# A transformer block on one core: the borders between its last four stages rearranged

## The chip, the cores and the metric

The kernel runs on one core of one Trainium2 chip. The core has a matrix engine (TensorE, PE), a vector engine (VectorE, DVE), a scalar engine (ScalarE, ACT), GpSimd (POOL) and queues that move data between device memory and the core's SBUF; almost all DMAs here are issued on SyncE's queue (SP). The metric is the device time of one execution in microseconds (us).

## The reference, cut to what matters

One block over 2048 latent tokens of width 1024, with 256 context tokens. `mix` is made of gated linear attention (GLA) and of differential softmax attention, 512 columns each; the rest is what the change touches:

```python
mix = jnp.concatenate([gla_merge(og, r, gla_norm_g[l]),
                       diff_merge(od, diff_norm_g[l], lam_init)], axis=-1) @ w_out[l]
x = x + gt1 * mix
x = x + gt2 * swiglu(modulate(x, norm2_g[l], sh2, sc2), w_ffn_in[l], w_ffn_out[l])

def swiglu(h, w_in, w_out):
    gate, up = jnp.split(h @ w_in, 2, axis=-1)     # hidden width 2816
    return (jax.nn.silu(gate) * up) @ w_out
```

`gt1` and `gt2` are vectors over the 1024 output columns, `diff_merge` is an RMS norm over each head's 128 columns.

## The kernel before, in words

All products are float32, made of three matmuls each (`mm3`, lines 93 to 96): every operand is split into a rounded high part and a low rest by `split` (lines 89 to 91), a copy on ACT (L90) and a subtraction on DVE (L87). The elementwise helpers `mul`, `add` and `sub` have lines 81, 84 and 87, so many groups of the trace carry those lines. The order of PE's instructions is the order in which the program emits them (`manual_schedule(engines=MS)`, MS holding PE alone); the other engines' order is set by the scheduler, which takes what its own model of time says is ready, by priority, that is by place in the program.

*Attention.* 64 tiles of 128 queries (4 heads x 16); scores `s` on PE, softmax on ACT, and `combine` takes one probability map from the other (`p`): a multiply on DVE and an addition on POOL. The AV stream transposes `p`, splits it (`ah`, `al`) and multiplies with the values; its last tiles run after the last scores.

*Out-projection.* w_out's eight tiles of 128 x 1024 are loaded into buffers of the pool `xt`, multiplied by `gt1` on POOL and split into `woh`, `wol`. Token tiles lt = 15 to 0 then go through three generators. `prep(lt)` loads attention's output, merges the GLA output (state update `S` on DVE, L940), normalizes each head (ACT squares L976, DVE scalings L986 of `mx`), transposes (`tp`) and splits into `mh`, `ml`. `main(lt)` does 16 steps of three matmuls, two output halves of eight steps; after each half DVE adds the residual (`xt<-mm,xt`), which gives x1. `mod2(g)` takes two finished tiles: square on ACT (L1023), scaling to `xn` on DVE (L1025), transposes on PE and the modulation on DVE, into `hb` (SBUF) or device memory. Where each piece stands among the 16 steps of `main` is in `PREP` and `MOD`: `prep(lt-1)` is emitted at steps 0, 7 and 13 of `main(lt)`, `mod2` of the two tiles before at steps 1, 8, 10, 12 and 14 of every second one.

*Gate/up.* A Strassen-like scheme: each pair of 128 hidden columns of gate and up over 1024 tokens (one item, n) is seven products of 12 matmuls each, from seven weight combinations (`weights`, split into `wh`, `wl`) and seven activation slots (`slots`, o0 to o6, split into `o0h`, `o0l`, ...). `finish` combines the seven results with DVE additions (`e`) and ACT copies and Silus, and stores to device memory (`act`). There are 44 items, 22 on each half of the tokens; the slots are built once for each half by `rebuild`, in items 0 and 21. Four of the seven products add into an accumulator bank that a product before has left there:

```python
SEQ_P = ((0, True), (1, True), (0, False), (2, True), (3, True), (2, False), (3, False))
```

The second column says whether a product opens its bank; before product 2 adds into bank 0, the result of product 0 must have been copied (`e1`, ACT), and before products 5 and 6 the sums of products 3 and 4 must have been made (DVE). `last_group` normalizes and modulates tiles 0 and 1 during item 1.

*Down projection.* 16 pairs of token tiles; for a pair, 22 hidden tiles of six matmuls. Weights are loaded as `wo` (raw, `wrp`), split to `wot` (`wop`) by `down_weights`; token chunks are loaded as `ar` and split to `ah`, `al` by `tokens`. A second set of weights (the other 512 output columns) is prepared in pairs 5 and 7.

Pools are placed in SBUF one after the other, and a pool's memory comes free when the tiles before it in that place have been read, so the order of the pools decides what a transfer waits for.

Of the kernel before, what the change touches and what calls it, by code (L numbers as in the profile page):

```python
# [11 lines left out]
F32 = mybir.dt.float32  # L12
# [22 lines left out]
ORD0, ORD1 = (4, 5, 6, 7, 0, 1, 2, 3), (3, 2, 4, 5, 6, 7, 0, 1)  # L35
PAD4 = 16
# [5 lines left out]
MS = {mybir.EngineType.PE}  # L42
BKL = (3, 6, 9, 12)
# [9 lines left out]
def dit_block(ctx: ExitStack, tc: tile.TileContext, x, c, cx, c_ctx, w_mod, b_mod, norm1_g, w_in, gate_up,  # L53
# [651 lines left out]

    with ExitStack() as st:
# [55 lines left out]
        def score_stream():  # L762
            later, ring = [], iter(range(64))
            for bi, (h, qb, i0, nq) in enumerate(blocks):
                as_[bi] = []
                for i in range(i0, i0 + nq):
# [5 lines left out]
                    for c_ in range(2):  # L772
                        mx = sm.tile([P, 5], F32, name="mx", tag="mx")
                        for j, (o0, n) in enumerate(CH):
# [5 lines left out]
                            if j == len(CH) - 1:  # L780
# [5 lines left out]
                                if c_ == 1:  # L786
                                    later.append([CD, combine(pr, ls)])
# [9 lines left out]
        def combine(pr, ls):  # L797
            def go():
# [13 lines left out]
        def av_stream():  # L812
            ats, po, ending = {}, None, []
            NB = len(blocks) * NKT
            for p in range(NB + LOOK + 4):
# [21 lines left out]
                if 0 <= a < NB:  # L837
# [55 lines left out]
    with ExitStack() as st:  # L893
        st6 = st.enter_context(ExitStack())
        h2p = st6.enter_context(tc.tile_pool(name="s45h", bufs=1, reuse_waits="tile"))
# [11 lines left out]
        pad = st1.enter_context(tc.tile_pool(name="s4pad", bufs=1, side="right"))  # L907
        G.memset(pad.tile([P, 56], F32, name="pad"), 0.0)
        gl = st1.enter_context(tc.tile_pool(name="s4g", bufs=2, side="right", reuse_waits="tile"))
        pp = st1.enter_context(tc.tile_pool(name="s4p", bufs=2, side="right", reuse_waits="tile"))  # L910
        pad = st1.enter_context(tc.tile_pool(name="s4pad2", bufs=1, side="right"))
        G.memset(pad.tile([P, PAD4], F32, name="pad"), 0.0)
# [3 lines left out]
        xp = st1.enter_context(tc.tile_pool(name="s4x", bufs=4, reuse_waits="tile"))  # L916
# [3 lines left out]
        gt1 = ph.tile([P, D], F32, name="gt1", tag="mh")  # L920
# [44 lines left out]
        def prep(lt):  # L965
# [3 lines left out]
            xt = xp.tile([P, D], F32, name="xt", tag="xt")  # L969
            load(xt, x[0, lt * P:(lt + 1) * P, :])  # L970
            gla_out(lt, mx[:, 0:512])
            sq = pp.tile([P, P], F32, name="sq", tag="sq", bufs=1)
# [14 lines left out]
            mh = ph.tile([P, KT, P], F32R, name="mh", tag="mh")  # L987
            ml = ph.tile([P, KT, P], F32R, name="ml", tag="ml")
# [28 lines left out]
        def mod2(g):  # L1017
            b, o0 = (g % 4) // 2, (g % 2) * 256
            xn = []
            for t in range(2):  # L1020
                n_t = wk.tile([P, D], F32, name="xn", tag="xn")
# [3 lines left out]
                V.tensor_scalar(out=n_t, in0=x1s[2 * g + t], scalar1=rs, scalar2=None, op0=ALU.mult)  # L1025
                xn.append(n_t)
            yield
            for kp in range(KT // 2):
# [4 lines left out]
                else:  # L1033
                    ht = wk.tile([P, 2, 256], F32, name="ht", tag="ht")
# [43 lines left out]
        pad = st6.enter_context(tc.tile_pool(name="s5pad", bufs=1, side="right"))  # L1078
        G.memset(pad.tile([P, 56], F32, name="pad"), 0.0)
# [240 lines left out]
```

## Time and profile before

| | |
|---|---|
| median of 3 runs | 3119.8 us (3116.95 to 3121.58) |
| profiled execution | 3118.64 us |
| its span | 3116.9 us, 41971 instructions |
| PE busy in the span | 3023.3 us (97%) |
| mean granted clock of TensorE | 0.988 of full speed |

The profile is of one execution; its times are from the span's start. PE is the matmul, PEld the loading of weights into the array beside it. A wait is idle time of an engine, with what ended it; a tile is named as in the program, buffer numbers left out, so `xt<-xt,gt` is an instruction that writes a buffer of `xt` and reads `xt` and `gt`. The granted clock has two levels, 1.2 and 2.4 GHz; 1.00 in a window is 2.4 GHz throughout.

### The profile page before, as it was taken

What the parts mean: (1) busy time and instruction counts of PE and PEld (TensorE: products, weight loads), DVE (VectorE), ACT (ScalarE), POOL (GpSimd) and SP (SyncE); (2) the same over time, 40 slices, a digit from 0 to 9 for tenths busy, and PEclk for the clock granted to TensorE, in tenths of its full rate; (3) what the DMA queues carried; (4) which work ended last, traced back from release to release, by engine and by line L of the source; (5) the groups of instructions that cost most, each with busy time, mean ns of one, the idle gap of its engine ahead of it and who ended that gap; (6) DMA issues with size and microseconds to landing.
All of it is one profiled execution on the core that took longest, in us unless ns stands there. A gap on an engine that the chain in (4) does not pass through costs nothing. (4 is left out here: it accounts for less than half of the span.)

```text
span 3116.9 us, 41971 instructions
## 1 busy us (share of the span) xinstructions
PE 3023.3 (97%) x15124; PEld 2486.5 (80%) x15124; DVE 2203.2 (71%) x4820; ACT 1411.9 (45%) x2195; POOL 495.6 (16%) x304
## 2 busy tenths in 40 slices
PE   7999999999989999999799899999999998999999
PEld 4888889888867777777588788888788887888887
DVE  7878667888889999999777676666766665424232
ACT  5333466666657777777434333333433333212121
POOL 2111100000046555555411000000000000000000
PEclk9999999999999999999899999999999999999999
DMA  8866511121141313121455442233233223545331
GB/s 310 291 236 220 177 66 67 60 95 64 53 130 35 90 35 90 35 75 28 135 180 171 150 144 82 83 88 89 86 89 89 84 81 124 192 144 175 120 134 68
DMA packets 319555, 363.47 MB, mean 117 GB/s; under 512 B 25842, under 2 KB 256691, under 8 KB 312691
## 3 DMA queue, kind: packets, MB, share of 16 engines
q1 hardware_dynamic: 316754, 351.36, 35.4%
q0 software_dynamic: 2304, 8.39, 0.8%
q8 instruction: 119, 1.95, 0.3%
q10 hardware_dynamic: 288, 1.05, 0.1%
q14 instruction: 90, 0.73, 0.1%
HBM read 249.96 MB, written 110.76 MB: 116 GB/s over the span
## 5 line engine op out<-in xcount | busy, mean ns | idle before, releaser
L84 POOL TENSOR_TENSOR p<-p,p 128x1152 f32<-128x1152 f32 x128 | 366.0, 2879 | 286.9 <-DVE p L808 124.6
L778 DVE TENSOR_SCALAR_CACHE_REDUCE p<-s 128x512 f32<-128x512 f32 (+1 forms) x640 | 381.8, 629 | 13.5 <-PE s L777 9.5
L94 PE MATMUL mm<-wh,hh 128*128 128x512 f32 (+2 forms) x976 | 379.0, 388 | 0.0
L96 PE MATMUL mm<-wh,hl 128*128 128x512 f32 (+2 forms) x976 | 355.1, 364 | 0.2 <-DVE hl L87 0.2
L95 PE MATMUL mm<-wl,hh 128*128 128x512 f32 (+2 forms) x976 | 354.1, 363 | 0.0
L84 DVE TENSOR_TENSOR e<-p,e 128x512 f32<-128x512 f32 x220 | 152.0, 691 | 225.7 <-PE p L96 225.4
L784 ACT ACTIVATE p<-p,nm 128x2304 f32<-128x2304 f32 x128 | 283.8, 2217 | 44.5 <-DVE nm L782 44.5
L776 PE MATMUL s<-k,qh 128*128 128x512 f32 (+1 forms) x640 | 275.5, 434 | 9.2 <-DVE p L778 8.5
L94 PE MATMUL o<-wot,ah 128*128 128x512 f32 x704 | 275.4, 391 | 6.8 <-ACT wot L90 6.1
L95 PE MATMUL o<-wot,ah 128*128 128x512 f32 x704 | 275.2, 391 | 0.9 <-DVE wot L87 0.9
L96 PE MATMUL o<-wot,al 128*128 128x512 f32 x704 | 275.0, 391 | 0.4 <-DVE al L87 0.4
L90 ACT ACTIVATE wh<-wi 128x512 fp32r<-128x512 f32 x172 | 108.4, 631 | 299.2 <-PE p L95 296.3
L777 PE MATMUL s<-k,ql 128*128 128x512 f32 (+1 forms) x640 | 234.3, 373 | 2.1 <-DMA ql<-ql 2.1
L90 ACT ACTIVATE ah<-ar 128x1408 fp32r<-128x1408 f32 x64 | 85.3, 1374 | 315.9 <-PE o L95 311.5
L96 PEld LDWEIGHTS mm<-wh,hl 128*128 128x128 f32 x976 | 184.8, 189 | 30.4 <-DVE hl L87 0.6
L94 PEld LDWEIGHTS mm<-wh,hh 128*128 128x128 f32 x976 | 186.1, 191 | 23.0 <-issue 0.5
L95 PEld LDWEIGHTS mm<-wl,hh 128*128 128x128 f32 x976 | 186.3, 191 | 21.5 <-issue 0.5
L87 DVE TENSOR_TENSOR al<-ar,ah 128x1408 fp32r<-128x1408 f32 x64 | 101.4, 1621 | 132.0 <-ACT ah L90 132.0
L90 ACT ACTIVATE wh<-s 128x512 fp32r<-128x512 f32 x129 | 81.5, 632 | 224.3 <-PE p L95 146.8
L821 PE MATMUL t<-ident,p 128*128 128x128 f32 x1152 | 174.7, 274 | 2.0 <-POOL p L84 2.0
L821 PEld LDWEIGHTS t<-ident,p 128*128 128x128 f32 x1152 | 142.7, 142 | 37.4 <-issue 4.1
L776 PEld LDWEIGHTS s<-k,qh 128*128 128x128 f32 x640 | 121.7, 190 | 59.7 <-DVE p L778 18.1
(295 smaller groups left out, 7112.2 us busy)
## 6 DMA issues: line engine op xcount, KB each, us to landing
ar<-act SPq DMA_DIRECT2D x64, 704.0 KB, 4.3
wi<-in_w_ffn_in SPq DMA_DIRECT2D x86, 512.0 KB, 5.1
act<-e SPq DMA_DIRECT2D x88, 256.0 KB, 4.2
wm<-in_w_mod SPq DMA_DIRECT2D x32, 512.0 KB, 4.9
xt<-in_x SPq DMA_DIRECT2D x30, 512.0 KB, 4.2
wr<-in_w_in SPq DMA_DIRECT2D x12, 1024.0 KB, 7.6
wo<-in_w_ffn_out SPq DMA_DIRECT2D x44, 256.0 KB, 5.3
hdh<-hh SPq DMA_DIRECT2D x9, 1024.0 KB, 4.8
```

What stands on the lines that cost most here:

```text
L84: (eng or V).tensor_tensor(out=o, in0=a, in1=b, op=ALU.add)
L87: (eng or V).tensor_tensor(out=o, in0=a, in1=b, op=ALU.subtract)
L90: S.activation(hi, src, AF.Copy)
L94: T.matmul(ps, a[0], b[0], start=start, stop=False, **how)
L95: T.matmul(ps, a[0], b[1], start=False, stop=False, **how)
L96: T.matmul(ps, a[1], b[0], start=False, stop=stop, **how)
L776: T.matmul(ps[:, 0:n], qd[0][c_][:, qc], ks_[h, c_][:, o0:o0 + n], start=True, stop=False)
L777: T.matmul(ps[:, 0:n], qd[1][c_][:, qc], ks_[h, c_][:, o0:o0 + n], start=False, stop=True)
L778: V.tensor_scalar(out=pr[c_][:, o0:o0 + n], in0=ps[:, 0:n], scalar1=1.0, scalar2=-3.0e38, op0=ALU.mult, op1=ALU.max, accum_out=mx[:, j:j + 1])
L784: S.activation(pr[c_], pr[c_], AF.Exp, bias=nm, accum_out=l)
L821: T.transpose(pt[:, i, :], as_[bi][i][:, kt * P:(kt + 1) * P], ident)
```

## The change

- *Attention to out-projection.* w_out isn't multiplied by `gt1` any more; instead `main` multiplies each output half by it (on DVE, in place in the accumulator). The raw tiles go to buffers of `xp`, `xnp` and `ph`, which lie elsewhere than before, and each split gets the priority of a place in the last AV block (`marks`). The last two `combine`s are done on DVE alone. `ORD0` and `ORD1`, the order of the steps in `main`, change.
- *Out-projection.* The squares of `prep` write into `mh` instead of a scratch; the head scalings and the `xn` scalings move from DVE to ACT.
- *Out-projection to gate/up.* The raw weights, the split weights and the temporaries of gate/up lie over buffers that come free before the out-projection's end; the first fetch and the first three weight combinations are raised in priority; the very first product does its high-by-high matmuls first and the ones with low parts after.
- *Gate/up and down projection.* `MS5` makes DVE and ACT issue in program order too.
- *Gate/up to down projection.* The first two token chunks are loaded and split in the last gate/up item; raw weight buffers go from 4 to 3, raw token buffers from 4 to 2, split weights from NH + 6 to NH + 2, x1t from 3 to 2; the second set of weights starts with 2 instead of 6 in pair 5.

```diff
-ORD0, ORD1 = (4, 5, 6, 7, 0, 1, 2, 3), (3, 2, 4, 5, 6, 7, 0, 1)
-PAD4 = 16
+ORD0, ORD1 = (4, 5, 6, 7, 3, 2, 1, 0), (0, 1, 2, 3, 4, 5, 6, 7)
 MS = {mybir.EngineType.PE}
+MS5 = {mybir.EngineType.PE, mybir.EngineType.DVE, mybir.EngineType.Activation}
...
+    marks = []
...
-                                    later.append([CD, combine(pr, ls)])
+                                    later.append([CD, combine(pr, ls, bi == len(blocks) - 1 and i >= i0 + nq - 2)])
...
-                    if e == 0:
+                    if e == 0 or last:
                         V.scalar_tensor_tensor(out=p0, in0=p1, scalar=cf, in1=p0, op0=ALU.mult, op1=ALU.add)
...
+                if p >= NB - NKT:
+                    marks.append(tc.cur_priority)
                 yield
...
-        gl = st1.enter_context(tc.tile_pool(name="s4g", bufs=2, side="right", reuse_waits="tile"))
-        pp = st1.enter_context(tc.tile_pool(name="s4p", bufs=2, side="right", reuse_waits="tile"))
...
-        ph = st1.enter_context(tc.tile_pool(name="s4h", bufs=2, side="right", reuse_waits="tile"))
+        xp = [st1.enter_context(tc.tile_pool(name=f"s4x{u}", bufs=2, side="right", reuse_waits="tile")) for u in range(2)]
+        xnp = st1.enter_context(tc.tile_pool(name="s4n", bufs=2, side="right", reuse_waits="tile"))
+        gp = st1.enter_context(tc.tile_pool(name="s4gt", bufs=1, reuse_waits="tile"))
+        htp = st1.enter_context(tc.tile_pool(name="s4ht", bufs=2, reuse_waits="tile"))
         wp = st1.enter_context(tc.tile_pool(name="s4w", bufs=1, reuse_waits="tile"))
+        ph = st1.enter_context(tc.tile_pool(name="s4h", bufs=2, reuse_waits="tile"))
+        pp = st1.enter_context(tc.tile_pool(name="s4p", bufs=2, reuse_waits="tile"))
+        gl = st1.enter_context(tc.tile_pool(name="s4g", bufs=2, reuse_waits="tile"))
...
-        for k in ORD0:
-            w = xp.tile([P, D], F32, name="xt", tag="xt")
+        for n, k in enumerate(ORD0):
+            pool, tag = {3: (xnp, "xn"), 2: (xnp, "xn"), 1: (ph, "mh"), 0: (ph, "ml")}.get(k, (xp[k // 2 % 2], "xt"))
+            w = pool.tile([P, D], F32, name="wr", tag=tag)
             load(w, w_out[0, k * P:(k + 1) * P, :])
-            mul(w, w, gt1, G)
-            split(wo[k][0], wo[k][1], w)
+            with tc.high_priority(offset=tc.cur_priority - marks[3 + 2 * n]):
+                split(*wo[k], w)
...
+            mh = ph.tile([P, KT, P], F32R, name="mh", tag="mh")
+            ml = ph.tile([P, KT, P], F32R, name="ml", tag="ml")
...
-                S.activation(sq, mx[:, 512 + h * P:512 + (h + 1) * P], AF.Square, accum_out=ss[:, h:h + 1])
+                S.activation(mh[:, h, :], mx[:, 512 + h * P:512 + (h + 1) * P], AF.Square, accum_out=ss[:, h:h + 1])
...
-                V.tensor_scalar(out=mx[:, hs], in0=mx[:, hs], scalar1=rs[:, h:h + 1], scalar2=None, op0=ALU.mult)
+                S.activation(mx[:, hs], mx[:, hs], AF.Copy, scale=rs[:, h:h + 1])
...
                     if k == order[-1]:
+                        mul(ps, ps, gt1[:, js])
                         add(x1[:, js], ps, xt[:, js])
...
-                V.tensor_scalar(out=n_t, in0=x1s[2 * g + t], scalar1=rs, scalar2=None, op0=ALU.mult)
+                S.activation(n_t, x1s[2 * g + t], AF.Copy, scale=rs)
...
+            if n == i == 0:
+                for u, v in ((wh_, 0), (wh_, 1), (wl_, 0)):
+                    for k in range(4):
+                        T.matmul(ps, u[:, k, :], slots[0][v][:, k, :], start=u is wh_ and v == k == 0,
+                                 stop=u is wl_ and k == 3)
+                return ps
...
-        with tc.manual_schedule(engines=MS):
-            fetch(0)
+        with tc.manual_schedule(engines=MS5):
+            with tc.high_priority(offset=100):
+                fetch(0)
+                for m in range(AHEAD):
+                    weights(*flat[m])
             fetch(1)
-            for m in range(AHEAD):
-                weights(*flat[m])
...
+                if n == len(work) - 1 and i in (0, 4):
+                    t = i // 4
+                    ar = rwp.tile([P, KT * 2 * P], F32, name="ar", tag="wi")
+                    tokens(8 + t, 0, ar[:, 0:HC * P].rearrange("p (j t) -> p j t", t=P),
+                           [h2p.tile([P, 2048], F32R, name=f"c{t}{u}", tag=f"hb{t}{u}")[:, 0:HC * P]
+                            .rearrange("p (j t) -> p j t", t=P) for u in range(2)])
...
-        wrp = st.enter_context(tc.tile_pool(name="s6r", bufs=4, reuse_waits="tile"))
-        op_ = st.enter_context(tc.tile_pool(name="s6o", bufs=3, reuse_waits="tile"))
+        op_ = st.enter_context(tc.tile_pool(name="s6o", bufs=2, reuse_waits="tile"))
+        wrp = st.enter_context(tc.tile_pool(name="s6r", bufs=3, reuse_waits="tile"))
+        arp = st.enter_context(tc.tile_pool(name="s6ar", bufs=2, reuse_waits="tile"))
         acp = st.enter_context(tc.tile_pool(name="s6a", bufs=4, reuse_waits="tile"))
-        wop = st.enter_context(tc.tile_pool(name="s6w", bufs=NH + 6, reuse_waits="tile"))
+        wop = st.enter_context(tc.tile_pool(name="s6w", bufs=NH + 2, reuse_waits="tile"))
...
-                        if n == 5 and j < 6:
+                        if n == 5 and j < 2:
                             down_weights(1, j)
-                        if n == 7 and j + 6 < NH:
-                            down_weights(1, j + 6)
+                        if n == 7 and j + 2 < NH:
+                            down_weights(1, j + 2)
```

## Rows read from the trace of the kernel before

**Rows 1.** Windows: length, busy us by engine (instructions), clock, DMA share, GB/s.

```profile
1500.00:1560.00 60.00, 41.90 (x178) 30.59 (x177) 42.36 (x61) 25.59 (x62) 17.75 (x10) 0.80 0.41 130
1600.00:1620.00 20.00, 20.00 (x107) 16.76 (x106) 18.59 (x45) 8.09 (x31) 1.87 (x2) 1.00 0.58 191
...
2620.00:2640.00 20.00, 11.79 (x36) 7.87 (x35) 13.39 (x15) 11.20 (x14) 0.00 (x0) 0.74 0.89 295
...
2177.80:2220.50 42.70, 40.30 (x170) 32.50 (x169) 37.75 (x35) 20.64 (x21) 0.00 (x0) 0.96 0.34 105
1762.40:1816.10 53.70, 44.61 (x186) 34.12 (x185) 49.58 (x65) 27.20 (x37) 0.53 (x1) 0.94 0.45 157
```

**Rows 2.** Timeline of PE, 1762 us: start, us, instruction.

```profile
1762.43 0.39 PE L94 MATMUL p<-o0h,wh 128*128 128x512 f32 x1
1762.66 0.39 PE L95 MATMUL p<-o0l,wh 128*128 128x512 f32 x1
```

**Rows 3.** Waits of PE, 1478 to 1560 us: total, times, longest.

```profile
PE mm L95 <- DVE wol L87: 8.9, 3, 8.0
PE o L95 <- DVE al L87: 5.1, 1, 5.1
PE mm L94 <- ACT woh L90: 4.0, 2, 3.3
PE t L821 <- POOL p L84: 2.0, 1, 2.0
```

**Rows 4.** Timeline, 1529 to 1552 us: start, us, instruction [idle before it].

```profile
1534.29 9.44 POOL L81 TENSOR_TENSOR xt<-xt,gt 128x1024 f32<-128x1024 f32 x4 [21.50 <-DVE wol L87]
...
1536.71 7.16 DVE L940 SCALAR_TENSOR_TENSOR S<-S,Tall,Ub 64x128 f32<-64x128 f32 x3
...
1529.59 0.80 PE L94 MATMUL mm<-woh,mh 128*128 128x512 f32 x1 [3.27 <-ACT woh L90]
...
1551.95 0.48 PE L94 MATMUL mm<-woh,mh 128*128 128x512 f32 x1
```

**Rows 5.** Lines by form, 1560 to 1740 us: busy, mean ns | idle before.

```profile
L976 ACT ACTIVATE sq<-mx 128x128 f32<-128x128 f32 x50 | 15.3, 306 | 13.6 <-DMA mx<-md 12.9
L1023 ACT ACTIVATE xn<-xt 128x1024 f32<-128x1024 f32 x14 | 14.7, 1050 | 10.6 <-DVE xt L84 10.6
L976 ACT ACTIVATION_READ_ACCUMULATOR sq<-mx 128x1 f32 x50 | 9.3, 187 | 0.0
...
L84 DVE TENSOR_TENSOR xt<-mm,xt 128x512 f32<-128x512 f32 x26 | 17.8, 686 | 0.5
...
L986 DVE TENSOR_SCALAR mx<-mx,rs 128x128 f32<-128x128 f32 x52 | 12.7, 280 | 0.1
...
L1025 DVE TENSOR_SCALAR xn<-xt,n_rs 128x1024 f32<-128x1024 f32 x12 | 9.0, 753 | 0.0
```

**Rows 6.** Timeline of DVE and of PE, 1603 to 1606 us.

```profile
1603.42 0.72 DVE L1025 TENSOR_SCALAR xn<-xt,n_rs 128x1024 f32<-128x1024 f32 x1
...
1605.70 0.60 PE L1038 MATMUL tp<-ident,xn 128*128 128x128 f32 x4
```

**Rows 7.** Waits of PE, 1762 to 1820 us, the three largest.

```profile
PE p L94 <- ACT wh L90: 3.0, 1, 3.0
PE p L95 <- DVE o4l L87: 2.3, 1, 2.3
PE p L96 <- DVE wl L87: 1.9, 2, 0.9
```

**Rows 8.** Timeline of DVE and of ACT, 2201 to 2205 us.

```profile
2201.42 2.28 DVE L87 TENSOR_TENSOR o4l<-hb,o4h 128x2048 fp32r<-128x2048 f32 x1
...
2203.01 1.90 ACT L90 ACTIVATE o5h<-hb 128x2048 fp32r<-128x2048 f32 x1
```

**Rows 9.** Tile `wot` on ACT, 2630 to 2660 us: duration ns min/median/max, first, last start.

```profile
L90 ACT ACTIVATE wot<-wo x18: 613/632/633, 2633.7 to 2659.6; 128x512 fp32r<-128x512 f32 x18
```

**Rows 10.** The page, part 6: issues, KB each, median us to landing.

```profile
wo<-in_w_ffn_out SPq DMA_DIRECT2D x44, 256.0 KB, 5.3
```

More of the change, by code (lines that the diff above doesn't have):

```diff
@@ L795, in score_stream, with combine @@
                 e[1]()
-        def combine(pr, ls):
+        def combine(pr, ls, last):
             def go():
@@ L919, in dit_block @@
         ps_mm = st1.enter_context(tc.tile_pool(name="s4mm", bufs=4, space=PSUM, reuse_waits="tile"))
-        gt1 = ph.tile([P, D], F32, name="gt1", tag="mh")
+        gt1 = gp.tile([P, D], F32, name="gt1")
         load(gt1, gt_d[0])
@@ L1020, in mod2 @@
             for t in range(2):
-                n_t = wk.tile([P, D], F32, name="xn", tag="xn")
+                n_t = xnp.tile([P, D], F32, name="xn", tag="xn")
                 ss = wk.tile([P, 1], F32, name="ss", tag="ss")
@@ L1033, in mod2 @@
                 else:
-                    ht = wk.tile([P, 2, 256], F32, name="ht", tag="ht")
+                    ht = htp.tile([P, 2, 256], F32, name="ht", tag="ht")
                 for j in range(2):
@@ L1077, in dit_block @@
         sl1 = st6.enter_context(tc.tile_pool(name="s5o", bufs=1, reuse_waits="tile"))
-        pad = st6.enter_context(tc.tile_pool(name="s5pad", bufs=1, side="right"))
-        G.memset(pad.tile([P, 56], F32, name="pad"), 0.0)
-        rwp = st6.enter_context(tc.tile_pool(name="s5r", bufs=2, side="right", reuse_waits="tile"))
+        rwp = rsk.enter_context(tc.tile_pool(name="s5r", bufs=2, side="right", reuse_waits="tile"))
         opp = st6.enter_context(tc.tile_pool(name="s5w", bufs=7, side="right", reuse_waits="tile"))
+        tmp = st6.enter_context(tc.tile_pool(name="s5t", bufs=1, side="right", reuse_waits="tile"))
         ep = st6.enter_context(tc.tile_pool(name="s5e", bufs=1, side="right", reuse_waits="tile"))
-        tmp = st6.enter_context(tc.tile_pool(name="s5t", bufs=1, side="right", reuse_waits="tile"))
         ps5 = st6.enter_context(tc.tile_pool(name="s5ps", bufs=2, space=PSUM, reuse_waits="tile"))
+        slots[6] = slot(sl1, 6)
         def rebuild(blocks, i, fresh):
@@ L1089, in rebuild @@
                 slots[i] = slot(sl0 if i < 2 else sl1, i)
-            if i == 1 and fresh:
+            if i == 1:
                 add(b11, b11, b12)
@@ L1192, in finish, with tokens @@
                 store(act_d[half][1][:, :, j, :], e["e2"].rearrange("p (t n) -> p t n", n=P))
-        flat = [(n, i) for n in range(len(work)) for i in range(7)]
-        with tc.manual_schedule(engines=MS):
-            fetch(0)
+        HC = NH // 2
+        downs, chunks = {}, {}
+        def tokens(lt, c_, ar, pair):
+            load(ar, act_d[lt // 8][lt // 4 % 2][:, lt % 4, c_ * HC:(c_ + 1) * HC])
+            split(*pair, ar)
+            chunks[lt, c_] = pair
+        flat = [(n, i) for n in range(len(work)) for i in range(7)]
+        with tc.manual_schedule(engines=MS5):
[3 more added lines that the diff above has]
+                    weights(*flat[m])
             fetch(1)
-            for m in range(AHEAD):
-                weights(*flat[m])
             late = last_group()
@@ L1202, in dit_block @@
                 if n == 0 and i < 5:
-                    rebuild(hb, i + 2, True)
+                    rebuild(hb, i + 2, i != 4)
                 if m + AHEAD < len(flat):
@@ L1239, in down_weights, with next_tokens @@
             downs[dd, j] = wt[:, 0], wt[:, 1]
-        def tokens(lt, c_):
-            ar = acp.tile([P, HC, P], F32, name="ar", tag="ar")
-            load(ar, act_d[lt // 8][lt // 4 % 2][:, lt % 4, c_ * HC:(c_ + 1) * HC])
-            chunks[lt, c_] = [acp.tile([P, HC, P], F32R, name=f"a{u}", tag=f"a{u}") for u in "hl"]
-            split(*chunks[lt, c_], ar)
+        def next_tokens(lt, c_):
+            tokens(lt, c_, arp.tile([P, HC, P], F32, name="ar", tag="ar"),
+                   [acp.tile([P, HC, P], F32R, name=f"a{u}", tag=f"a{u}") for u in "hl"])
         pairs = [(dd, lt) for dd in range(2) for lt in (*range(8, 16, 2), *range(0, 8, 2))]
-        with tc.manual_schedule(engines=MS):
+        with tc.manual_schedule(engines=MS5):
             for n, (dd, lt) in enumerate(pairs):
@@ L1251, in dit_block @@
                 ps, x1t = [], []
-                for t in range(2):
-                    ps.append(ps6.tile([P, 512], F32, name="o", tag="o"))
-                    x1t.append(op_.tile([P, 512], F32, name="x1t", tag="x1t"))
-                    load(x1t[t], x1_d[lt + t][:, js])
                 for c_ in range(2):
+                    nx = (n, 1) if c_ == 0 else (n + 1, 0)
                     if n == 0 and c_ == 0:
-                        for t in range(2):
-                            tokens(lt + t, 0)
-                    if n == 0:
-                        for j in range(c_ * HC, (c_ + 1) * HC):
+                        for j in range(HC):
                             down_weights(0, j)
-                    nx = (n, 1) if c_ == 0 else (n + 1, 0)
                     if nx[0] < len(pairs):
                         for t in range(2):
-                            tokens(pairs[nx[0]][1] + t, nx[1])
+                            next_tokens(pairs[nx[0]][1] + t, nx[1])
+                    if n == 0 and c_ == 0:
+                        for j in range(HC, NH):
+                            down_weights(0, j)
+                        gt2 = gtp.tile([P, D], F32, name="gt2")
+                        load(gt2, gt_d[1])
+                    if c_ == 0:
+                        for t in range(2):
+                            ps.append(ps6.tile([P, 512], F32, name="o", tag="o"))
+                            x1t.append(op_.tile([P, 512], F32, name="x1t", tag="x1t"))
+                            load(x1t[t], x1_d[lt + t][:, js])
                     for j in range(c_ * HC, (c_ + 1) * HC):
```

20 lines of the change are left out of this document (6 added, 14 removed).

## The prediction

> **What bounds the kernel now.** I read the page first: TensorE is busy nearly throughout, so nothing but its idle and slow stretches can be won. The windows say where they are: at the borders between stages [rows 1]. From 1500 to 1560 us (attention into out-projection) PE works 41.9 of 60 us at a mean granted clock of 0.80; from 1762.4 to 1816.1 (the first two items of gate/up) 44.6 of 53.7 at 0.94; from 2177.8 to 2220.5 (its items 21 and 22) 40.3 of 42.7 at 0.96; from 2620 to 2640 (into the down projection) 11.8 of 20 at 0.74. In the out-projection's steady part PE is full, but two things there matter for the change: DVE is nearly full too (18.6 of 20), and ACT is not (8.1 of 20).
>
> Then the waits of PE, border by border. At the first, 20.0 us go to the splits of w_out (`wol` 8.9, `woh` 4.0), an `al` split 5.1 and POOL's combine 2.0 [rows 3]. The timeline tells why: POOL multiplies w_out by the gate, 4 tiles in 9.44 us, and while it does, three small `S` updates (64x128) on DVE take 7.16 us, as long as ten 128x512 additions; the second half of w_out gets its gate only from 1534.29, after POOL waited 21.5 us for the first half's `wol`, and so the 24 matmuls of lt=15's first output half last from 1529.59 to 1551.95 [rows 4]. At the second border 9.1 us are idle, 7.2 of them in front of splits of weights and slots [rows 1, 7]; in the middle of gate/up it is 2.4 us, at the third border 8.2 [rows 1]. A 512-column matmul has a pitch of 0.227 us at full clock [rows 2] (24 of them, one output half, would be 5.4 us), so a gate/up item of 84 takes 19.04 us: that is the yardstick.
>
> **Border 1: removed.** Idle time there is 20.0 us. A mean clock of 0.80 over 60 us is 24 us at 1.2 GHz and the rest at 2.4; some 9 of the 24 are idle anyway; the other 15 us of matmuls would take 7.5. Together 27.5. After the change w_out lies in buffers that attention doesn't use, is loaded before and split in gaps of the last AV block: 8 x 1.05 us on ACT (its 128x1024 square [rows 5]) and 8 x 1.2 on DVE (half a 2048-wide one and a little, [rows 8]), against 34 us of ACT's time and 18 of DVE's that are free from 1500 to 1560 [rows 1]. POOL's multiplies are gone, and so is the slow `S`; the last two combines move to DVE, 2 x 2 instructions, an estimate of 1.25 us each for 1152 columns from the 2.28 us of 2048 [rows 8]. I keep 0.9 us for the first output transposes and the first mh split: gain 27 us, so the second half (j=1) of lt=15 starts near 1525 instead of 1551.95. Bounds: 23 (the combines delay some `al` splits), 30 (those 0.9 us are hidden too, and the splits' own instructions leave the path).
>
> **Out-projection: added.** The gate on the output is 32 DVE multiplies of 0.69 us (the 128x512 add has 686 ns [rows 5]), 22 us; the 64 `mx` scalings (280 ns) and 16 `xn` copies (753 ns) leave DVE, 30 us. So DVE gets lighter by 8 us in all, and the gate costs only as latency: 0.65 us on x1. What bites is ACT's order. The squares of `prep(lt-1)`, issued in main(lt), now write into `mh`, which has two buffers, so they can't start before main(lt+1) has read its last `mh`, which is when main(lt) begins; before, they wrote into a scratch and could run an iteration ahead. In the seven iterations with `mod2` the time until the `xn` transposes now has to hold on ACT: 4 squares with their accumulator reads (306 + 187 ns each, 1.9 us), 4 scalings (an estimate of 1.0 from the 306 ns) and 2 `xn` copies at 1.05 instead of 0.75 us. With 0.65 for the gate that is 4.15 us more in a chain that ended 1.56 us before PE came (the copy ended at 1604.14, the transpose began at 1605.70 [rows 6]). At most 2.6 us of wait each; nothing, if ACT does the `xn` copies ahead of the squares. About 1.1 us (the x1 square of the tile finished earlier) can go ahead, so 1.5 to 1.6 each: 7 x 1.6 = 11 us. Bounds 2 and 20.
>
> The rows give 753 ns on DVE and 1050 ns on ACT for 128x1024 [rows 5], while DVE is full and ACT is at 8 of 20. The Trainium skill, "ScalarE: Activation LUTs", section "Rules for kernel authors", says to put multiplications on VectorE, not ScalarE, which speaks against this move. By that rule the two copies cost 0.6 us per iteration, 4 us in all and with nothing gained; by the row on DVE's load they may be free, and the order of the queue decides, not the duration. My 11 us is worked out without the rule.
>
> **Border 2.** The first gate/up weights are loaded and split before the last out-projection tile ends, and the first product takes its low halves last. Today's waits for wl, wh (0.9, 3.0, 0.9) and the half clock behind them (0.94 over 53.7 us is 6.4 us at 1.2 GHz, nearly 6 of it work: 2.9) go: 7.7 us. Against that stands the new order: in gate/up DVE and ACT now issue in program order (`MS5`), as PE does already. For item 0 I listed both queues in that order with the durations of the trace (a 2048-wide instruction takes 2.28 us on DVE and 1.90 on ACT [rows 8], back to back 2.2 and 1.8; a 512-wide one 0.69, back to back 0.6, on ACT 0.5): product 4 waits 4.0 us for its slot, whose ACT split is behind the `e1` copy and slot 3; product 5 waits 6.9 for the sum `f3` (PE adds into the bank that `f3` reads), which stands behind slot 5's subtraction and split, `s2` and a weight split; item 1 waits 5.1 for `lxn`, whose squares stand behind the Silu of item 0; the two long ones bring half clock, at 2.8 each. Items 0 and 1 take 60.7 us instead of 53.6: +7 (3 to 10).
>
> **Middle of gate/up: moved by the order alone.** Items 21 and 22 (seven new slots, 10 instructions of 2.2 us on DVE) take 42.7 us together now, 4.6 more than two steady items; the scheduler puts the sums that PE waits for between the slots' splits, and 2.4 us of waits remain [rows 1]. In program order: after product (21,1) ends, DVE does the rest of slot 0's split and a weight (2.7), f1 (0.6), the slot-1 addition (2.2), waits for ACT's 1.8, then o1l 2.2, wl5 0.6, o2l 2.2, s2 0.6, wl6 with its wait 1.2, f3 0.6: f3 ends 14.9 us after, PE wants it after 3 products, 8.2. Wait 6.8. Product (22,2) needs item 22's `e1` copy, which ACT has behind slot 5, f6, Silu and slot 6: 7.1 more. Each leaves half clock (as the wait of today does, clock 0.96 in that window [rows 1]), 2.8 us: 57.7 instead of 42.7, +15 (10 to 18). What is late next is nothing: from item 23 DVE has some 11 of 19 us to do.
>
> **Border 3.** Token chunks and the first weights are ready when the last product ends: the 12 us lost up to 2640 (8.2 idle; 0.74 over 20 us is 10.4 at 1.2 GHz, some 8 of it work: 4) go. But raw weight buffers drop from 4 to 3. Four gave 18 weights from 2633.7 to 2659.6 [rows 9], 1.5 us each, a cycle of 6 us; three would give 2.0, or 1.9 as the first chunks' 1.4 MB no longer fall into this stretch, and PE eats one in 6 x 0.227 = 1.36. Some 8 weights can be split ahead; the other 14 fall behind by 14 x 0.55 = 8 us. Net -4. Bounds -9 (a cycle of 5 us) and +4 (a load lands in 5.3 us [rows 10], with issue and two splits 7: 2.3 a weight). Fewer ar and x1t buffers: hidden, since a chunk lasts 2 x 11 x 3 x 0.227 = 15 us and is loaded one ahead.
>
> **Sum**: -27 + 11 + 7 + 15 - 4 = +2 us on the profiled 3118.6, that is 3120.6; the median lies 1.2 above the profiled run, which is inside the spread of the three runs. I say 3121. About 0.2% (6.2 us) is what a measurement of this kernel can tell from no change.
>
> **Rivals.**
> - *Faster: program order costs no more than today's.* If the sums f3 and e1 come in time (f3 within 8.2 us of product (21,1)), the middle costs 0 and border 2 wins its 7.7: -27 + 11 - 8 + 0 - 4 = -28, 3091; with half of these waits, 3106. For it: DVE has 37.8 us of work [rows 1] in the 38 us of items 21 and 22, so a good order exists. Against: today's order, chosen freely, still loses 4.6 us there, and the new one leaves DVE idle while ACT splits slot 1. 0.36 for all cases that end under 3113.6.
> - *Slower: the down weights run dry.* At 2.3 us a weight 14 x 0.95 = 13 us, and three of the waits as long as the one that lowered the clock in the middle, 2.8 each: 22 instead of 8, so 3135. It decides from 2.1 us a weight on. For it: DMA engines are 89% busy there [rows 1], and the splits wait for loads. Against: the first chunks' 1.4 MB no longer fall into that stretch. 0.18. Stage 4 at its upper bound (2.6 us a time, clock lowered) gives 3130 to 3140: 0.08.
> - *Border 1 does not move.* If splits of w_out do not get into the last AV block (DVE is at 42 of 60 there [rows 1]), j=0 still waits for them: 8 x 1.2 us, and the gain shrinks to about 17; all in place as before: 3147. 0.05.
> - Forecast, within 6.2 us of before: 0.33.
>
> Range: 3097 to 3140, from the larger part of the faster rival to beyond the slower one; the likeliest case alone 3113 to 3127. Faster 0.36, same 0.33, slower 0.31.
>
> **What would show it.** Right: j=1 of lt=15 starts near 1525; no POOL multiply of w_out; PE waits of 1 to 2 us for `tp<-xn` in odd tiles; first product without waits, then waits of 4 to 7 us for `e`; items 21 and 22 near 28 us each with PE waiting on `e`; no gap before the first down matmul, then waits for `wot` on loads `wo`. Wrong: items 21 and 22 near 20 us (the order isn't what I listed), or j=1 after 1535, or no waits in the out-projection.

## The result, and the profile after

The changed kernel takes 3142.18 us (median of 4 runs, 3141.57 to 3142.61), the kernel before 3118.38 (3115.69 to 3121.58): a ratio of 1.0076, 95% interval 1.0058 to 1.0093. It is slower by 24 us, above the range of 3097 to 3140. The profiled execution took 3141.57 us, its span is 3139.8.

Where TensorE starts the same piece of work in both traces (us from the span's start) gives the account:

| stretch | before | after | difference | predicted |
|---|---|---|---|---|
| second output half of lt=15 starts | 1551.95 | 1531.77 | -20.2 | -27 |
| from there to the first gate/up product | 210.5 | 226.2 | +15.7 | +11 |
| items 0 and 1 of gate/up | 53.6 | 66.1 | +12.5 | +7 |
| items 2 to 20 | 361.8 | 361.8 | 0 | 0 |
| items 21 and 22 | 42.7 | 58.9 | +16.2 | +15 |
| items 23 to the last up product (o6 of item 43) | 397.1 | 397.1 | 0 | 0 |
| from there to the last down matmul | 493.7 | 492.0 | -1.7 | -4 |
| sum | | | +22.4 | +2 |

Every term has the sign that was forecast, and every one came out worse than forecast: items 21 and 22 by 1 us, the other four by 2 to 7. First the windows that answer to [rows 1] (length, busy us by engine and instructions, clock, DMA share, GB/s): the first border, the out-projection, items 0 and 1, items 21 and 22, the third border.

```profile
1500.00:1560.00 60.00, 54.37 (x271) 43.36 (x269) 41.88 (x85) 33.46 (x93) 5.21 (x5) 0.94 0.53 163
1600.00:1620.00 20.00, 18.32 (x93) 14.93 (x92) 16.27 (x37) 12.02 (x32) 2.42 (x3) 1.00 0.56 184
1757.90:1824.00 66.10, 50.39 (x185) 38.27 (x184) 47.23 (x59) 27.01 (x34) 0.53 (x1) 0.85 0.43 143
2185.80:2244.60 58.80, 43.16 (x169) 34.63 (x168) 38.49 (x36) 20.22 (x20) 0.00 (x0) 0.85 0.12 36
2641.70:2700.00 58.30, 52.89 (x211) 41.14 (x211) 29.58 (x36) 22.43 (x30) 0.00 (x0) 0.94 0.64 207
```

At the first border PE is busy 54.4 of 60 us at 0.94, against 41.9 at 0.80 [rows 1]. The out-projection, full before, now has PE idle 1.7 of 20 us, DVE lighter (16.3 after 18.6) and ACT heavier (12.0 after 8.1). In the two stretches of gate/up PE is idle 15.7 and 15.6 us, at a clock of 0.85.

**First border.** The waits of PE (total, times, longest) from 1478 to 1560 us, answering to [rows 3]:

```profile
PE tp L1000 <- DVE mx L81: 4.0, 1, 4.0
PE o L95 <- DVE al L87: 1.7, 2, 1.4
PE tp L1044 <- ACT xn L1031: 1.5, 1, 1.5
```

No wait for `woh`, `wol` or POOL is left, as forecast. The wait for `mx` was not in the sum. The timeline of PE and of DVE shows its chain (start, us, instruction, idle before it and what ended it):

```profile
1503.84 0.60 PE L957 MATMUL gm<-S,qq 128*128 128x128 f32 x4
...
1516.09 0.61 PE L957 MATMUL gm<-S,qq 128*128 128x128 f32 x4
...
1516.74 0.69 DVE L84 TENSOR_TENSOR kk<-gm,kk 128x512 f32<-128x512 f32 x1 [1.27 <-PE gm L957]
...
1521.03 0.69 DVE L81 TENSOR_TENSOR mx<-vv,kk 128x512 f32<-128x512 f32 x1
...
1521.78 1.11 PE L1000 MATMUL tp<-ident,mx 128*128 128x128 f32 x4 [3.96 <-DVE mx L81]
1522.55 0.78 PE L94 MATMUL mm<-woh,mh 128*128 128x512 f32 x1
...
1531.77 0.48 PE L94 MATMUL mm<-woh,mh 128*128 128x512 f32 x1
```

The GLA merge of lt=15 begins with eight matmuls `gm`; in PE's order four stand at 1503.84 and the other four only behind the last AV matmul. The merge is a chain of small steps over DVE and ACT, from 1516.1 to 1521.7, and PE has nothing else to do for most of it. In the kernel before the same merge was over at 1507.9, well ahead of its transposes at 1524.59; its inputs had been loaded at 896 us (the load of `S` and the chain's last step, before, then the load of `S` after):

```profile
895.81 0.55 SPq L933 DMA_DIRECT2D S<-sf  x1
1507.21 0.68 DVE L81 TENSOR_TENSOR mx<-vv,kk 128x512 f32<-128x512 f32 x1
```

```profile
1491.33 0.45 SPq L939 DMA_DIRECT2D S<-sf  x1
```

So the merge was not late before; the change made it late. Pool `gl`, which holds these inputs, moved from the right side of SBUF to the left (see the change), and at 894 us the changed kernel loads w_out instead. That the move is why the inputs come some 595 us later is read from the edit and the rows, no run moved the pool back; and PE's order adds its part, as a run below shows. Behind the 4.0 us wait the first matmul takes 0.78 us where later ones take 0.39: half clock, till about 1527.

**Out-projection.** In every second token tile PE now waits 1.5 to 1.7 us for the second `xn` copy, 10.8 us in seven waits, and once 3.4 us for the head half of `mx`; the kernel before waited 1.6 us in the same iteration, but at its GLA half. One of the seven, on ACT and on PE (compare [rows 6], where the copy was done 1.56 us before PE came):

```profile
1638.19 0.31 ACT L983 ACTIVATE mh<-mx 128x128 fp32r<-128x128 f32 x1 [0.56 <-PE mm L95]
...
1642.96 1.27 ACT L993 ACTIVATE mx<-mx,rs 128x128 f32<-128x128 f32 x4
1644.14 1.14 ACT L1031 ACTIVATE xn<-xt,n_rs 128x1024 f32<-128x1024 f32 x1
...
1646.35 1.15 ACT L1031 ACTIVATE xn<-xt,n_rs 128x1024 f32<-128x1024 f32 x1 [0.31 <-DVE n_rs L144]
...
1647.55 0.55 PE L1044 MATMUL tp<-ident,xn 128*128 128x128 f32 x3 [1.51 <-ACT xn L1031]
```

The first square waits for PE's matmul that reads the `mh` it overwrites, and the scalings of `mx` stand ahead of the copies: the chain on ACT that was forecast.

**Items 21 and 22.** The two waits of PE, then DVE's queue behind the first and ACT's behind the second:

```profile
2206.75 0.77 PE L94 MATMUL p<-o5h,wh 128*128 128x512 f32 x1 [7.22 <-DVE e L84]
2227.99 0.80 PE L94 MATMUL p<-o2h,wh 128*128 128x512 f32 x1 [8.42 <-ACT e L1187]
```

```profile
2193.93 0.68 DVE L84 TENSOR_TENSOR e<-p,e 128x512 f32<-128x512 f32 x1
2194.53 2.28 DVE L84 TENSOR_TENSOR hb<-hb,hb 128x2048 f32<-128x2048 f32 x1
2198.85 2.29 DVE L87 TENSOR_TENSOR o1l<-hb,o1h 128x2048 fp32r<-128x2048 f32 x1 [2.04 <-ACT o1h L90]
2201.06 0.69 DVE L87 TENSOR_TENSOR wl<-wi,wh 128x512 fp32r<-128x512 f32 x1
2201.66 2.28 DVE L87 TENSOR_TENSOR o2l<-hb,o2h 128x2048 fp32r<-128x2048 f32 x1
2203.87 0.69 DVE L87 TENSOR_TENSOR s<-wi,s 128x512 f32<-128x512 f32 x1
2205.31 0.69 DVE L87 TENSOR_TENSOR wl<-s,wh 128x512 fp32r<-128x512 f32 x1 [0.76 <-ACT wh L90]
2205.92 0.68 DVE L84 TENSOR_TENSOR e<-p,e 128x512 f32<-128x512 f32 x1
```

```profile
2225.03 0.63 ACT L1202 ACTIVATE e<-e 128x512 f32<-128x512 f32 x1 [2.96 <-DVE e L84]
2225.56 1.89 ACT L90 ACTIVATE o6h<-hb 128x2048 fp32r<-128x2048 f32 x1
2227.36 0.58 ACT L1187 ACTIVATE e<-p 128x512 f32<-128x512 f32 x1
```

The DVE rows are the list of the prediction, instruction by instruction: f1, the slot-1 addition, 2.04 us of idle until ACT has split slot 1, o1l, wl, o2l, s, wl, and only then f3, for which PE has been waiting. On ACT the `e1` copy stands behind the Silu and the split of slot 6, as listed. The waits are 7.2 and 8.4 us against 6.8 and 7.1 forecast. In the six runs below that keep gate/up in program order and the slots where they are, the two items take 57.3 to 57.8 us (57.7 forecast), so 58.9 is at the upper end.

**Second border.** SP issues the first gate/up load at 1748.20, behind the last stores of `h`; ACT splits the first weight at 1752.88, so it has landed by then; DVE stands idle 4.0 us, does the last gate multiply of the out-projection first, and the low part and the sums of the first weights come after it (SP, ACT, DVE, PE):

```profile
1748.20 15.65 SPq L1138 DMA_DIRECT2D wi<-in_w_ffn_in  x4
```

```profile
1752.88 0.63 ACT L90 ACTIVATE wh<-wi 128x512 fp32r<-128x512 f32 x1 [6.88 <-DMA wi<-in_w_ffn_in]
```

```profile
1758.13 0.70 DVE L81 TENSOR_TENSOR mm<-mm,gt 128x512 f32<-128x512 f32 x1 [4.01 <-PE mm L96]
...
1759.48 0.68 DVE L87 TENSOR_TENSOR wl<-wi,wh 128x512 fp32r<-128x512 f32 x1
1760.08 0.69 DVE L87 TENSOR_TENSOR s<-wi 128x512 f32<-128x512 f32 x1
```

```profile
1762.93 0.63 PE L94 MATMUL p<-o1h,wh 128*128 128x512 f32 x1 [1.50 <-ACT wh L90]
1775.73 0.51 PE L94 MATMUL p<-o4h,wh 128*128 128x512 f32 x1 [2.51 <-ACT o4h L90]
1778.06 0.80 PE L95 MATMUL p<-o4l,wh 128*128 128x512 f32 x1 [1.82 <-DVE o4l L87]
1787.81 0.76 PE L94 MATMUL p<-o5h,wh 128*128 128x512 f32 x1 [4.69 <-DVE e L84]
1803.62 0.33 PE L1122 MATMUL p<-ident,lxn 128*128 128x128 f32 x1 [4.54 <-DVE lxn L1115]
```

So the first two products, which were to lose nothing, take 5.0 and 4.5 us instead of 2.7; the other waits are the listed ones. They leave half clock behind four places, not two: the granted clock is 0.62 from 1762.9 to 1767.4, 0.69 from 1775.7 to 1787.8, 0.50 to 1793.0 and 0.68 from 1803.6 to 1808.9.

**Third border.** The first down matmul starts 2.0 us after the end of the last up product; in the kernel before it was 6.1 us. The first split of `wot` stands on ACT behind the last Silu, though the first three loads of `wo` were issued between 2628.94 and 2633.2:

```profile
2645.38 0.63 ACT L1202 ACTIVATE e<-e 128x512 f32<-128x512 f32 x1 [7.40 <-DVE e L84]
2645.92 1.65 ACT L90 ACTIVATE wot<-wo 128x512 fp32r<-128x512 f32 x3
```

Then come waits for `wot` and `al` of 3.5 us in all, the last at 2686.

### The profile page after: what moved, and what is told of

It is laid out like the page before. It is cut to its first block, busy times and chain, and to the rows that moved or that the text cites. A ratio compares the mean times of both kernels' runs of the same rounds, so it can differ in the third digit from the quotient of the medians.

```text
span 3139.8 us, 41871 instructions
## 1 busy us (share of the span) xinstructions
PE 3033.0 (97%) x15124; PEld 2492.8 (79%) x15124; DVE 2197.4 (70%) x4774; ACT 1422.0 (45%) x2273; POOL 463.8 (15%) x290
## 4 chain that ended last, share of the span: by engine, by line
PE 64%; DVE 3%; ACT 2%; DMA 1%; issue 1%; POOL 0%; SPq 0%; DVEq 0%; ACTq 0%; POOLq 0%
PE p L94 8%; PE p L95 8%; PE p L96 8%; PE o L95 6%; PE o L96 6%; PE o L94 6%; PE s L777 4%; PE s L778 4%; PE t L822 4%; PE o L845 3%; PE mm L94 2%; PE mm L96 2%; PE mm L95 2%; DMA wo<-in_w_ffn_out 1%; POOL p L84 0%
## 5 line engine op out<-in xcount | busy, mean ns | idle before, releaser
L84 POOL TENSOR_TENSOR p<-p,p 128x1152 f32<-128x1152 f32 x124 | 354.9, 2883 | 283.3 <-DVE p L809 175.8
L95 PE MATMUL o<-wot,ah 128*128 128x512 f32 x682 | 266.3, 390 | 1.5 <-DVE wot L87 1.5
L94 PE MATMUL o<-wot,ah 128*128 128x512 f32 x682 | 265.9, 390 | 0.9 <-ACT wot L90 0.9
L96 PE MATMUL o<-wot,al 128*128 128x512 f32 x682 | 266.2, 390 | 0.5 <-DVE al L87 0.5
L87 DVE TENSOR_TENSOR wl<-s,wh 128x512 fp32r<-128x512 f32 x129 | 88.9, 690 | 115.1 <-ACT wh L90 115.1
L777 PEld LDWEIGHTS s<-k,qh 128*128 128x128 f32 x640 | 122.4, 191 | 57.6 <-DVE p L779 15.7
```

What stands on the lines that cost most here:

```text
L84: (eng or V).tensor_tensor(out=o, in0=a, in1=b, op=ALU.add)
L87: (eng or V).tensor_tensor(out=o, in0=a, in1=b, op=ALU.subtract)
L94: T.matmul(ps, a[0], b[0], start=start, stop=False, **how)
L95: T.matmul(ps, a[0], b[1], start=False, stop=False, **how)
L96: T.matmul(ps, a[1], b[0], start=False, stop=stop, **how)
L777: T.matmul(ps[:, 0:n], qd[0][c_][:, qc], ks_[h, c_][:, o0:o0 + n], start=True, stop=False)
```

## The experiments

Times of single runs (no interval given) are of one execution, beside the median of the kernel before on the same chip, 3117.4 to 3118.9 us; their verdicts rest on stretches of the trace, as in the table above. Stretches ahead of the one in question shift by some 3 us between runs.

**Program order of DVE and ACT.** One kernel gives it up in the changed kernel, in gate/up and in the down projection (the line stands at both); another adds it alone to the kernel before, by the reverse edit:

```diff
-        with tc.manual_schedule(engines=MS5):
+        with tc.manual_schedule(engines=MS):
```

> The changed kernel with DVE and ACT left to the scheduler again in gate/up and in the down projection (only PE in program order). Theory A: the program order of DVE and ACT is what costs time in items 0, 1, 21 and 22 of gate/up. Then items 21 and 22 take 42 to 44 us together (58.9 in the changed kernel), items 0 and 1 take 46 to 54 (66.1), and the time is 3105 to 3118 us. Theory B: the loss in items 0 and 1 comes from the new places and priorities of weights and buffers, and only items 21 and 22 suffer from the order. Then items 0 and 1 stay above 60 us and the time is 3122 to 3130.

3120.49 us (ratio to before 1.0008, 0.9999 to 1.0018). Items 21 and 22 take 42.3 us, as Theory A has it; items 0 and 1 take 55.5, 1.5 us above its range and well under Theory B's 60. The time is 2.5 us above Theory A's range. In the trace the first gate/up product starts 3.3 us later than in the changed kernel: PE waits 3.3 us for `wh`, which the scheduler puts behind the splits of three slots on ACT. The third border loses 3.6: the first down matmul again comes 9.3 us late, where the changed kernel lost 2.0.

```profile
PE o L94 <- ACT wot L90: 9.3, 1, 9.3
```

> The kernel before with one part of the change alone: DVE and ACT in program order in gate/up and in the down projection. Theory A: items 21 and 22 take 57 to 60 us instead of 42.7 and items 0 and 1 take 58 to 64 instead of 53.6, so the time is 3137 to 3147 us. Theory B: items 0 and 1 stay at 53 to 55, the time is 3132 to 3137.

3152.4 us (ratio 1.0110, 1.0095 to 1.0125), above both ranges. Items 21 and 22 take 57.7 us, as Theory A has it; items 0 and 1 take 69.1, 5 us above its range. They lose 15.6 us by the order, as the waits for the late weights (`wh` 3.0, `wl` 0.9) stay beside the new ones. The third border does not gain by the order alone: from the last up product to the last down matmul it takes 496.5 us, 2.8 more than before. Its waits for `e` in items 21 and 22 are those of the changed kernel:

```profile
PE p L95 <- ACT e L1176: 7.9, 1, 7.9
PE p L95 <- DVE e L85: 7.2, 1, 7.2
```

**The place of the sums in the queue.** In the changed kernel a slot is rebuilt three products later:

```diff
+                if n == NH and i < 3:
+                    rebuild(hb0, i + 4, True)
                 ps = product(n, i)
                 finish(n, i, ps)
-                if n == NH - 1:
-                    rebuild(hb0, i, True)
+                if n == NH - 1 and i >= 3:
+                    rebuild(hb0, i - 3, True)
```

> The changed kernel with the rebuilding of a slot emitted three products later, so that in program order the sums of item 21 stand ahead of the splits of slots 1 to 3. Theory A: the waits come from the place of the sums in DVE's and ACT's queues; then item 21 takes 19 to 20 us (28.2), item 22 30 to 34 (30.7), and the time falls by 4 to 9 us. Theory B: the two items take what DVE's work takes, whatever the order; then they stay at 57 to 60 us together.

Item 21 takes 19.04 us, no wait at all, item 22 33.2 with waits of 10.2 for `e1` and 1.8 for a sum: 52.2 together, and 3136.1 us. Theory A: the same work on DVE (38.5 us in both) costs PE 6.7 us less when the sums stand elsewhere.

**The squares and the copies on ACT.**

```diff
+            sq = pp.tile([P, P], F32, name="sq", tag="sq", bufs=1)
...
-                S.activation(mh[:, h, :], mx[:, 512 + h * P:512 + (h + 1) * P], AF.Square, accum_out=ss[:, h:h + 1])
+                S.activation(sq, mx[:, 512 + h * P:512 + (h + 1) * P], AF.Square, accum_out=ss[:, h:h + 1])
```

> The changed kernel with the squares of prep written into a scratch tile again instead of mh. Theory A: the seven waits of 1.5 us in front of the transposes of xn come from these squares, which can no longer run ahead and stand on ACT before the xn copies; then the waits shrink from 10.8 us in total to under 4 and the time falls by 7 to 12 us. Theory B: they come from the xn copies being on ACT at all (longer, and behind other ACT work); then 9 us or more of the waits stay and the time stays within 3 us of the changed kernel.

3128.85 us, which is 13.3 less than the changed kernel, more than the 7 to 12 of Theory A; the first gate/up product starts at 1745.9 instead of 1757.9, and the out-projection's stretch takes 215.8 us instead of 226.2. The waits for `xn` shrink from 10.8 to 1.9 us (Theory A):

```profile
PE tp L1045 <- ACT xn L1032: 1.9, 3, 0.8
```

```diff
-                S.activation(n_t, x1s[2 * g + t], AF.Copy, scale=rs)
+                V.tensor_scalar(out=n_t, in0=x1s[2 * g + t], scalar1=rs, scalar2=None, op0=ALU.mult)
```

> The changed kernel with the two xn scalings on DVE again, the squares still in mh. Theory A (the squares hold up ACT): the chain gets shorter by 2 x 0.3 us and by what stood before the copies on ACT, so the waits in front of the transposes of xn shrink to between 3 and 7 us from 10.8. Theory B (the copies on ACT): the waits vanish, under 1 us in total.

3133.41 us, the stretch takes 219.9. The waits are 3.6 us, inside Theory A's range, with seven of them still there:

```profile
PE tp L1044 <- DVE xn L1031: 3.6, 7, 1.0
```

Undoing the squares takes away 8.9 of the 10.8 us, undoing the copies 7.2, so the two shares do not add up: the wait needs both, and with either undone the chain has about the length that PE needs. The third part of it, the gate multiply ahead of x1, was undone in no run. On ACT the copy takes 1140 ns, on DVE it took 753 [rows 5]. The Trainium skill, "ScalarE: Activation LUTs", section "Rules for kernel authors", puts multiplications on VectorE; that agrees with this run, where the copies back on DVE make the stretch 6.3 us shorter, more than the 4 us that the durations alone had given.

**The GLA merge of lt=15.**

```diff
-            gla_out(lt, mx[:, 0:512])
+            with tc.high_priority(offset=tc.cur_priority - marks[8]) if lt == NT - 1 else ExitStack():
+                gla_out(lt, mx[:, 0:512])
```

> The changed kernel with the GLA merge of lt=15 given the priority of a place inside the last AV block, so that its matmuls run before the AV stream ends. Theory A: the wait of 4.0 us in front of the transposes of mx, and the half clock behind it, are all that is missing of the predicted gain at the first border; then the second output half of lt=15 starts at 1524 to 1526 (1531.8 in the changed kernel) and the time falls by 6 to 8 us. Theory B: another wait takes its place; then it starts after 1529 and the time falls by less than 3.

PE's order is that of the program inside a stage; this priority moves the merge's matmuls among those of the stage before. The second half of lt=15 starts at 1527.57, 4.2 us earlier, and the time is 3137.68: between the two theories. The wait of 4.0 is gone with the half clock behind it, and one of 0.5 for `on` takes its place. The last AV matmul starts at 1518.31 here, at 1515.87 in the changed kernel, so 2.4 us are lost ahead of the border.

**Raw weight buffers.**

```diff
-        wrp = st.enter_context(tc.tile_pool(name="s6r", bufs=3, reuse_waits="tile"))
+        wrp = st.enter_context(tc.tile_pool(name="s6r", bufs=4, reuse_waits="tile"))
```

> The changed kernel with 4 instead of 3 raw buffers for the down weights. Theory A: three raw buffers set the pace of the weights; then the waits for wot behind the first one vanish (3.4 us with the half clock they leave) and the stretch from the start of the last up product to the last down matmul falls from 492.0 to 486 to 488 us. Theory B: the pace is that of the transfers and the splits' order; then that stretch stays within 2 us of 492.

The stretch takes 485.2 us instead of 492.0, 0.8 under Theory A's range, the time is 3134.32: Theory A, though 1.1 us of waits for `wot` stay behind the first. The three buffers cost 6.8 us (8 were forecast): 2.4 of waits, and the rest by the clock that they lower (1.00 here from 2641 to 2690, 0.84 to 1.00 in the changed kernel). The gap is clear of noise: the other six kernels with three buffers and the same down projection take 491.1 to 493.5. Behind the border 11 loads take 16.14 us to issue with three buffers and 12.04 with four, 1.5 and 1.1 us each (SP's timeline of the changed kernel, then of this one). The 22 splits of `wot` come every 1.67 us with three and every 1.34 with four; the 1.9 of the prediction was too slow:

```profile
2647.38 16.14 SPq L1261 DMA_DIRECT2D wo<-in_w_ffn_out  x11
```

```profile
2646.96 12.04 SPq L1261 DMA_DIRECT2D wo<-in_w_ffn_out  x11
```

**The first weight sums on POOL.**

```diff
-                sub(s3, a11, a21)
-                add(a21, a21, a22)
-                sub(s2, a21, a11)
+                ge = G if n == 0 else V
+                ge.tensor_tensor(out=s3, in0=a11, in1=a21, op=ALU.subtract)
+                add(a21, a21, a22, ge)
+                ge.tensor_tensor(out=s2, in0=a21, in1=a11, op=ALU.subtract)
```

> The changed kernel with the three weight sums of gate/up's item 0 (s, wi, s) made on POOL instead of DVE. Theory A: the first two products of item 0, which take 5.0 and 4.5 us instead of 2.7 each, are late because these sums stand on DVE behind the gate multiply and the residual of the last out-projection half, although their data landed before; on POOL they run before those, the wait of 1.5 us for wh and the half clock behind it go, and products 0 and 1 take under 6.5 us together, items 0 and 1 61 to 64 us instead of 66.1. Theory B: the weights landed too late for that (the first load is issued 9.7 us before the first product); then products 0 and 1 stay above 8.5 us together.

3143.88 us; products 0 and 1 take 12.3 us, in Theory B's range. This decides nothing about when the weights landed: on POOL the sums stood behind the store of the last x1 tile, began later than on DVE and took 1.3 us each instead of 0.7.

```profile
1760.44 0.53 POOL L1020 DMA_DIRECT2D x<-xt  x1 [10.05 <-DVE xt L84]
1760.99 1.30 POOL L1153 TENSOR_TENSOR s<-wi 128x512 f32<-128x512 f32 x1
```

**What the runs point to.** First gate/up left to the scheduler (the down projection in program order) and the squares in a scratch tile; then also the copies on DVE, the early GLA merge and four raw buffers, with the edits shown above:

> The changed kernel with two parts undone: DVE and ACT are left to the scheduler in gate/up (the down projection keeps program order), and the squares of prep go into a scratch tile. Theory A: the costs found so far add up, 12 us from the squares, 10 in items 0 and 1 and 16 in items 21 and 22, and the border to the down projection keeps its short gap (down starts 4 to 6 us after the last product begins): 3100 to 3108 us, faster than the kernel before. Theory B: the short gap needs gate/up in program order too; then down starts 10 to 13 us after the last product begins and the time is 3108 to 3116.

3105.27 us (ratio 0.9965, 0.9951 to 0.9979): Theory A. The down projection starts 4.9 us after the beginning of the last up product, as in the changed kernel, so of the two stages only the down projection has to keep the order for the short gap. The order is not enough for it: added alone to the kernel before, it leaves a gap of 10.7 us.

> What the runs so far point to, together: the changed kernel with gate/up's DVE and ACT left to the scheduler, the squares in a scratch tile, the xn scalings on DVE, the GLA merge of lt=15 early and four raw buffers for the down weights. If the savings add up, 3105.3 (the first two alone) less 4.5, 6.8 and about 1 gives 3092 to 3097 us, under the kernel before by 0.7%. If the waits that remain only change places, it stays at 3100 to 3106.

3091.41 us (ratio 0.9915, 0.9902 to 0.9929): faster than both kernels, 0.6 under the range, and the savings add up. The second output half of lt=15 starts at 1524.04, with the last AV matmul at 1515.04. What is left is mostly at the second border, where with the scheduler's order the slots' splits stand ahead of the first weights:

```profile
PE p L94 <- ACT wh L90: 7.4, 1, 7.4
PE p L1174 <- ACT wh L90: 3.3, 1, 3.3
```

## Why the prediction was wrong

The mechanisms that the prediction listed did show, place by place. The sum of +2 was wrong by 20 us because all five terms were too kind, four of them by 2 to 7 us, each by something that was not listed.

- *Border 1, 7 us short.* The step that failed is "I keep 0.9 us for the first output transposes and the first mh split". It took the GLA merge of lt=15 to be as early as in the kernel before (over at 1507.9) and put the move of its pool at nothing. Shown: the merge ends at 1521.7 and PE waits 4.0 us for it; 4.2 us come back when it is early, and with the other edits of the best kernel the second half starts at 1524.04, the whole gain that was forecast. Which of those edits brings the last 3.5 us no run takes apart, and such places shift by some 3 us between runs.
- *Out-projection, 4.7 us short.* The 7 x 1.6 us came out as 10.8 (the copies are 14, seven times two, not 16, but the wait does not go by that). Left out was the iteration with the extra slot work (lt=6): "PE is full" was read from 1600 to 1620 only, and in that iteration, at 1680, the kernel before waits 1.6 us for `mx`. Now it is 3.4, with a clock of 0.94 from 1640 to 1670. The squares in `mh` make it: with the squares in a scratch tile this wait is gone and one of 2.2 is back at the GLA half, as in the kernel before; with the copies on DVE the 3.4 stay.
- *Border 2, 5.5 us short.* Two steps failed. "Today's waits for wl, wh and the half clock behind them go: 7.7 us": 1.8 us of these waits stay, with the half clock behind them, as the first load was issued at 1748.20, behind the `h` stores, and DVE made the sums behind the last gate multiply. That the queue's order is what made the weights late is read from the rows; the run meant to show it decided nothing. And "the two long ones bring half clock, at 2.8 each": four places do. PE's idle time, 15.7 us, met the 16.0 that were listed, but partly by luck: the listed waits are 13.6 (2.5, 1.8, 4.7, 4.5), and those in front of the first weights fill the rest. What is left of the 66.1 us behind the idle time, two items of 19.04 and some 1.4 of transposes is 11 us, against 5.6. The working does not add up either: -7.7 + 16.0 + 5.6 is +13.9, near the 12.5 measured; +7 takes the other waits of the kernel before (o4, `e`, `lxn`, 4.2 us) as gone too, which is not said.
- *Items 21 and 22.* Right: 16.2 against 15, by the listed waits (the steps up to f3 add up to 14.7 us, not 14.9). Adding the order alone costs it (57.7), giving it up removes it (42.3), and moving the sums moves the wait.
- *Border 3, 2.3 us short.* Net -1.7 for -4. The buffers cost 6.8 us (8 forecast). The 12 us that were to go did not all go: with four buffers the stretch is 8.6 us shorter than before. The step that failed is "Some 8 weights can be split ahead": none was, because `wot`'s first split is queued on ACT behind the last Silu, and the start cost 2.0 us that the prediction had at nothing.
- *The rivals.* The faster one (order costs nothing) fell at once: PE waited 7.2 us for f3. The slower one (weights run dry) did not happen either: a weight came every 1.67 us, and it needed 2.1. The time passed even its end, by a sum of misses that no rival held. The terms' own upper bounds, -23 + 20 + 10 + 18 + 4, add up to +29, that is 3148; the range ended at 3140, as if they could not all come out badly together. At three of the five places the same kind of thing was left out: a chain that became the next one PE waits for once the known wait was gone.

## What to carry to other kernels

When a wait goes, look for the chain that PE meets next, and cost it before counting the gain. When a pool moves to make room for one transfer, look up what loses its early place: here w_out came early and the GLA merge's inputs came late. Taking an engine's order from the scheduler is a change to every stretch of that region: against the scheduler's order, in the changed kernel, it gained 4 us at the third border and 3 in front of the first gate/up product and cost 27 in two other stretches. Limiting it to the stage that needs it kept the gain of 4. A tile reused as scratch saves memory, but its owner's last reader becomes a wait for the engine that writes the scratch.

## What the runs showed of the hardware

Three `S` updates on DVE took 7.16 us, 2.39 each, while POOL multiplied w_out at 9.44 us for four, 2.36 each [rows 4]: each small DVE instruction lasted as long as a POOL one. In the changed kernel, with POOL idle, four take 1.16:

```profile
1517.46 1.16 DVE L946 SCALAR_TENSOR_TENSOR S<-S,Tall,Ub 64x128 f32<-64x128 f32 x4
```

The Trainium skill, "SBUF — State Buffer", describes the port pair that VectorE and GpSimd share as a lock held for a whole instruction (section "SBUF: two separate sides"); the two traces agree, 2.39 against 2.36 us.

The granted clock fell to half behind waits of 4.0 and 4.5 us as behind those of 7 to 8; behind the waits of 1.5 us in the out-projection it stayed at 1.00 (window 1600 to 1620). The length of one wait does not settle it: behind the 1.5 us in front of the second gate/up product, which came after one of 0.3, it was 0.62 (1762.9 to 1767.4).
